# Expert retrieval with dense gate operands and merged token halves in a two-layer decoder trunk

## Chip, cores and metric

One core of a Trainium2 chip. The metric is the device time of one execution of the whole program in microseconds, median of the runs.

## What is computed

Two layers over 256 tokens of width 1024. Each has a mixing sublayer (three head groups, one output projection) and an expert sublayer, each followed by a LayerNorm of the residual. The change concerns the expert sublayer alone:

```python
q = (xc @ wq).reshape(c, PEER_HEADS, 2, half)
sc = jnp.einsum('thid,ikd->thik', q, keys)
top_s, top_i = lax.top_k(sc, PEER_TOPK)
...
gate = jax.nn.softmax(best_s, axis=-1)
ue = u[idx]
ve = v[idx]
act = jax.nn.gelu(jnp.einsum('td,thkd->thk', xc, ue))
return jnp.einsum('thk,thkd->td', (gate * act), ve)
```

There are 128 x 128 experts and 8 x 16 = 128 of them are chosen per token. The kernel does not gather: it multiplies every token with all 16384 expert rows, multiplies the result with a gate that is zero for all but the chosen ones, and multiplies with all value rows.

## The kernel before, in words

**Precision and the weight stream.** All large products are done in three parts of fp32r: the high half of the weights times the high half of the activations, high times low, low times high. Every weight tile of 128 x 1024 comes from HBM (SP's queue, four buffers `raw`), `pump_split` (lines 107 to 122) writes its high half `hi` on ScalarE (L117) and its low half `lo = raw - hi` on VectorE or, for the tiles in `on_pool` (lines 89 to 92), on GpSimd (L118). It runs two tiles ahead of TensorE (`LOOK`); `hi` and `lo` have three buffers each.

**The expert sublayer** (`peer`, lines 821 to 1037). First come the queries and the key scores. Then the *first product*: 128 key blocks j, each one expert tile `("u", l, j)` times the transposed hidden state (`hTh`, `hTl`: 8 chunks of 128 x 256 tokens each), 24 matmuls of 256 columns (`proj_T`, lines 334 to 346). Two blocks share a PSUM bank `acc` of 2 x 256 floats. After each pair `uevac` (line 973) applies the gelu.

Beside the blocks runs background work, written as generators that `bg.step` moves on: `routing` for each half of the tokens (the top-16 searches on VectorE, L846 to L850, then the one-hot work that gives each chosen expert's row and column, `ijT`, and gate, `gT`), and, from about block 55, `wgen` (line 961): 64 gate steps of four tokens, one per block. A step makes one-hot matrices of row and column by comparing with a constant ramp (`gates`, L937, L940, L942, on VectorE), multiplies them on TensorE so that a 128 x 128 gate matrix per token stands in PSUM (`wmm`, two half-float matmuls per token, for the high and the low half of the gate), and multiplies that into `act`, the 128 x 128 x 256 activations (`apply`: L956 on VectorE for the blocks that are already evacuated; L958 on ScalarE writes the bare gate for those to come, and `uevac` then multiplies the gelu into it, L977 and L978).

```python
DVE.tensor_tensor(eq, iota4[:, None, :, :].to_broadcast(sh),
                  ijT[:, :, None, t0:t0 + TG].to_broadcast(sh), op=OP.is_equal)
...
mm(ps[:, i, :], A[:, 0, :, i], eq[:, 1, :, i], True, False)
```

The token is the innermost index of these tiles, so TensorE reads its operands with a step of four half floats.

The *second product* (from line 996) multiplies `act`, split in halves by `gsplit` (L1011 on ScalarE, L1012 on VectorE), with the 128 value tiles in matmuls of 512 columns. The first two pairs of halves live in the buffers of `eq` and `ga`, the others in the space of `hTh` and `hTl`.

**What sets the order.** Each engine executes its instructions in one fixed order, which a scheduler makes when the program is built, from the order in the code and its own idea of when each instruction is ready. So the code does not show where an instruction stands in its engine's queue; the listings in the section on the change do.

Of the kernel before, what the change touches and what calls it, by code (L numbers as in the profile page):

```python
# [46 lines left out]
def trunk(ctx, tc, x, wst, ut, vr, pp_d, rb_d, lnrow, bd_d, keys_d, out):  # L47
# [42 lines left out]
    for l in range(DEPTH):  # L90
        on_pool.update(index["w", l, i] for i in (0, 1, 14, 16, 18, N_IN + N_OUT, N_IN + N_OUT + 1))
        on_pool.update(index["u", l, j] for j in range(4, 110, 3))
# [57 lines left out]
    iota4 = const.tile([128, 128, 4], F16, name="iota4")  # L150
# [19 lines left out]
    def make_consts():  # L170
        POOL.iota(iota4, pattern=[[1, 128], [0, 4]], base=0, channel_multiplier=0, allow_small_or_imprecise_dtypes=True)
# [30 lines left out]
    def layer_norm(h, pool, pre, gb, store, nxt=None, final=False, after=None):  # L202
        """h [128, 2, D] in place, stored to store; returns the transposed split operands."""
# [13 lines left out]
    def layer_norm_(h, pool, pre, g, b, store, nxt, final, after):  # L217
        hT = None
        if not final:
            hTh = hpool.tile([128, KD, SEQ], F32R, name="hTh")  # L220
            hTl = hpool.tile([128, KD, SEQ], F32R, name="hTl")
            hT = (hTh, hTl)
# [84 lines left out]
    # (step, token block, part): r residual and sums, m mean and squares, v variance, n reciprocal root, s centre and  # L307
    # gain, o scale and bias with the transposes, l low halves, p the next weight pieces
# [25 lines left out]
    def proj_T(w, hT, ps, first=False):  # L334
        hi, lo = w
        hTh, hTl = hT
# [22 lines left out]
    def log1p_exp_neg_abs(pool, o, xin, n, tag):  # L359
        """o = max(x, 0) + log1p(exp(-|x|)) on [128, n]"""  # L360
# [32 lines left out]
    def mixer(l, mix, h, hT, pre):  # L393
        hTh, hTl = hT
# [5 lines left out]
        # small per-layer values  # L400
# [31 lines left out]
        # causal depthwise convolution  # L432
# [293 lines left out]
        # projection schedule  # L726
# [60 lines left out]
        # output projection  # L787
# [33 lines left out]
    def peer(l, pool, hT):  # L821
        hTh, hTl = hT
# [29 lines left out]
        def routing(tb):  # L852
# [73 lines left out]
            ACT.activation(gT[:, 1, ts], gr, AF.Copy, scale=LS)  # L926
# [4 lines left out]
        GS, LS = float(2 ** 15), float(2 ** 11)  # L931
# [41 lines left out]
        def uevac(jp_, ps):  # L973
            j = jp_ * 2
            t = state["t"]
            if t > 0:
                ACT.activation(ps[:, :, 0:t], ps[:, :, 0:t], AF.Gelu)  # L977
                DVE.tensor_tensor(act[:, j:j + 2, 0:t], act[:, j:j + 2, 0:t], ps[:, :, 0:t], op=OP.mult)  # L978
            if t < SEQ:
                ACT.activation(act[:, j:j + 2, t:SEQ], ps[:, :, t:SEQ], AF.Gelu)  # L980
# [169 lines left out]
```

## Time and profile before

| | |
|---|---|
| runs | 2100.47, 2103.36, 2103.90 us; median 2103.36 |
| profiled execution, first to last instruction (no other time of it is given) | 2106.6 us |
| busy: TensorE | 2030.2 us |
| busy: VectorE | 1548.2 us |
| busy: ScalarE | 1062.8 us |
| busy: GpSimd | 238.3 us |

How to read it: an engine's busy time is the time in which it executes an instruction; TensorE's matmuls overlap, so its busy time is not a measure of how well it is used. Times in rows are in us from the start of the span, the means of groups in ns. In rows PE is TensorE, PEld its weight loads, DVE VectorE, ACT ScalarE, POOL GpSimd. "[0.21 <-DVE act L956]" behind a row says how long the engine was idle before it and what ended that.

### The profile page before, as it was taken

What the parts mean: (1) busy time and instruction counts of PE and PEld (TensorE: products, weight loads), DVE (VectorE), ACT (ScalarE), POOL (GpSimd) and SP (SyncE); (2) the same over time, 40 slices, a digit from 0 to 9 for tenths busy, and PEclk for the clock granted to TensorE, in tenths of its full rate; (3) what the DMA queues carried; (4) which work ended last, traced back from release to release, by engine and by line L of the source; (5) the groups of instructions that cost most, each with busy time, mean ns of one, the idle gap of its engine ahead of it and who ended that gap; (6) DMA issues with size and microseconds to landing.
All of it is one profiled execution on the core that took longest, in us unless ns stands there. A gap on an engine that the chain in (4) does not pass through costs nothing. (4 is left out here: it accounts for less than half of the span.)

```text
span 2106.6 us, 33808 instructions
## 1 busy us (share of the span) xinstructions
PE 2030.2 (96%) x13212; PEld 1835.5 (87%) x13212; DVE 1548.2 (73%) x2713; ACT 1062.8 (50%) x1523; POOL 238.3 (11%) x120
## 2 busy tenths in 40 slices
PE   7999889999999999999989999899999999999998
PEld 6887889999999888888888769899999998888886
DVE  8786697379999655555687867963999995555555
ACT  5576455454443544444566755554444344444444
POOL 3100122222220000000010001222222200000000
PEclk9999999999999999999999999999999999999999
DMA  6434445544434666666654335455444446666665
GB/s 206 136 110 150 152 152 168 180 141 140 132 130 135 195 194 194 192 194 195 197 180 139 108 133 170 155 173 174 140 132 134 136 151 190 193 196 192 195 195 170
DMA packets 95919, 344.84 MB, mean 164 GB/s; under 512 B 11680, under 2 KB 11952, under 8 KB 95760
## 3 DMA queue, kind: packets, MB, share of 16 engines
q1 hardware_dynamic: 95552, 342.27, 50.3%
q8 instruction: 103, 1.69, 0.3%
q0 software_dynamic: 208, 0.42, 0.1%
q14 instruction: 56, 0.46, 0.1%
HBM read 339.51 MB, written 3.15 MB: 163 GB/s over the span
## 5 line engine op out<-in xcount | busy, mean ns | idle before, releaser
L118 DVE TENSOR_TENSOR lo<-raw,hi 128x1024 fp32r<-128x1024 f32 x544 | 677.5, 1246 | 383.9 <-ACT hi L117 383.5
L117 ACT ACTIVATE hi<-raw 128x1024 fp32r<-128x1024 f32 x630 | 663.8, 1056 | 452.2 <-PE acc L193 342.5
L193 PE MATMUL acc<-hTh,lo 128*128 128x256 f32 x2048 | 581.8, 284 | 20.1 <-DVE lo L118 18.8
L193 PE MATMUL acc<-hTh,hi 128*128 128x256 f32 x2048 | 592.0, 289 | 0.2 <-ACT hi L117 0.2
L193 PE MATMUL acc<-hTl,hi 128*128 128x256 f32 x2048 | 580.1, 283 | 0.0
L193 PEld LDWEIGHTS acc<-hTh,lo 128*128 128x128 f32 x2048 | 392.1, 191 | 24.3 <-DVE lo L118 22.4
L193 PE MATMUL acc<-hi,hTl 128*128 128x512 f32 x1056 | 411.4, 390 | 0.0
L193 PE MATMUL acc<-hi,hTh 128*128 128x512 f32 x1056 | 411.2, 390 | 0.0
L193 PE MATMUL acc<-lo,hTh 128*128 128x512 f32 x1056 | 411.1, 389 | 0.0
L193 PEld LDWEIGHTS acc<-hTh,hi 128*128 128x128 f32 x2048 | 394.3, 193 | 0.7 <-ACT hi L117 0.4
L193 PEld LDWEIGHTS acc<-hTl,hi 128*128 128x128 f32 x2048 | 392.8, 192 | 0.1
L118 POOL TENSOR_TENSOR lo<-raw,hi 128x1024 fp32r<-128x1024 f32 x86 | 223.6, 2602 | 1046.7 <-ACT hi L117 1015.7
L193 PEld LDWEIGHTS acc<-hi,hTh 128*128 128x128 f32 x1056 | 198.3, 188 | 41.6 <-issue 0.7
L193 PEld LDWEIGHTS acc<-hi,hTl 128*128 128x128 f32 x1056 | 198.2, 188 | 41.1
L193 PEld LDWEIGHTS acc<-lo,hTh 128*128 128x128 f32 x1056 | 198.3, 188 | 41.1
L193 PE MATMUL w<-hTh,hi 128*128 128x256 f32 x560 | 161.4, 299 | 7.5 <-DVE y L495 5.7
L1011 ACT ACTIVATE hTh<-act 128x512 fp32r<-128x512 f32 x124 | 77.7, 631 | 166.2 <-PE acc L193 166.2
L1012 DVE TENSOR_TENSOR hTl<-act,hTh 128x512 fp32r<-128x512 f32 x124 | 85.4, 693 | 97.4 <-ACT hTh L1011 97.4
L193 PE MATMUL w<-hTh,lo 128*128 128x256 f32 x560 | 156.9, 289 | 0.0
L193 PE MATMUL w<-hTl,hi 128*128 128x256 f32 x560 | 155.4, 287 | 0.0
L958 ACT ACTIVATE act<-w 128x272 f32<-128x272 f32 (+32 forms) x128 | 61.1, 478 | 146.5 <-DVE act L956 145.8
L193 PE MATMUL w<-eq,ga 128*128 128x128 f16 x512 | 128.0, 294 | 6.9 <-DVE ga L940 6.9
(268 smaller groups left out, 2323.5 us busy)
## 6 DMA issues: line engine op xcount, KB each, us to landing
raw<-in_ut SPq DMA_DIRECT2D x256, 512.0 KB, 3.5
raw<-in_vr SPq DMA_DIRECT2D x256, 512.0 KB, 3.5
raw<-in_wst SPq DMA_DIRECT2D x118, 512.0 KB, 3.5
raw<-in_lnrow SPq DMA_DIRECT2D x8, 512.0 KB, 3.6
hd<-h SPq DMA_DIRECT2D x4, 512.0 KB, 3.9
raw<-hd SPq DMA_DIRECT2D x4, 512.0 KB, 3.5
h<-in_x SPq DMA_DIRECT2D x2, 512.0 KB, 5.7
y<-in_lnrow SPq DMA_DIRECT2D x2, 512.0 KB, 7.0
```

What stands on the lines that cost most here:

```text
L117: ACT.activation(hi, raw, AF.Copy)
L118: (POOL if n in on_pool else DVE).tensor_tensor(lo, raw, hi.bitcast(F32), op=OP.subtract)
L193: PE.matmul(ps, lhsT, rhs, start=start, stop=stop)
L958: ACT.activation(v[:, :, c:128], ps[:, :, c:128], AF.Copy, scale=1.0 / GS)
L1011: ACT.activation(gh, src, AF.Copy)
L1012: DVE.tensor_tensor(gl, src, gh.bitcast(F32), op=OP.subtract)
```

## The change

Five edits in the expert sublayer:

1. The two halves of the hidden state become one tile `hT` with the halves side by side, and a new `proj_U` multiplies the high half of an expert chunk with both in one matmul of 512 columns, and its low half with the high half of the tokens in one of 256. A block now fills a whole PSUM bank: the first 256 columns hold high times high plus low times high, the others high times low.
2. `uevac` therefore copies the second half to SBUF (`us`, ScalarE) and adds the first (VectorE) for each block, and works on the sum in `us`.
3. `gates` makes dense tiles: per token one comparison and two comparisons with product, each a tensor_scalar of 128 half floats with the token's row, column or gate as scalars per partition, from a single ramp `iota1`. 12 instructions on VectorE take the place of 3. The low half of the gate is kept without the factor 2^11, so the third tile that undid it is gone.
4. GpSimd makes the low halves of two expert tiles in three for blocks 2 to 49, where it made those of one in three for blocks 4 to 109 (32 per layer in place of 36).
5. The buffers that the second product borrows first are those of `us` and `ga`, in place of `eq` and `ga`.

```diff
-        on_pool.update(index["u", l, j] for j in range(4, 110, 3))
+        on_pool.update(index["u", l, j] for j in range(2, 50) if j % 3)
...
-            hTh = hpool.tile([128, KD, SEQ], F32R, name="hTh")
-            hTl = hpool.tile([128, KD, SEQ], F32R, name="hTl")
-            hT = (hTh, hTl)
+            hT = hpool.tile([128, KD, 2, SEQ], F32R, name="hT")
+            hTh, hTl = hT[:, :, 0, :], hT[:, :, 1, :]
...
-            eq = pool.tile([128, 2, 128, TG], F16, name="eq", bufs=2)
-            A = pool.tile([128, 3, 128, TG], F16, name="ga", bufs=2)
-            sh = [128, 2, 128, TG]
-            DVE.tensor_tensor(eq, iota4[:, None, :, :].to_broadcast(sh),
-                              ijT[:, :, None, t0:t0 + TG].to_broadcast(sh), op=OP.is_equal)
-            DVE.tensor_tensor(A[:, 0:2], eq[:, 0:1].to_broadcast(sh), gT[:, :, None, t0:t0 + TG].to_broadcast(sh),
-                              op=OP.mult)
-            DVE.tensor_scalar(A[:, 2], eq[:, 1], 1.0 / LS, None, op0=OP.mult)
+            eq = pool.tile([128, TG, 128], F16, name="eq", bufs=2)
+            A = pool.tile([128, TG, 2, 128], F16, name="ga", bufs=2)
+            for i in range(TG):
+                ii, jj = (ijT[:, c, t0 + i:t0 + i + 1] for c in range(2))
+                DVE.tensor_scalar(eq[:, i, :], iota1, jj, None, op0=OP.is_equal)
+                for c in range(2):
+                    DVE.tensor_scalar(A[:, i, c, :], iota1, ii, gT[:, c, t0 + i:t0 + i + 1], op0=OP.is_equal, op1=OP.mult)
...
-                mm(ps[:, i, :], A[:, 0, :, i], eq[:, 1, :, i], True, False)
-                mm(ps[:, i, :], A[:, 1, :, i], A[:, 2, :, i], False, True)
+                for c in range(2):
+                    mm(ps[:, i, :], A[:, i, c, :], eq[:, i, :], c == 0, c == 1)
...
+        def proj_U(w, ps):
+            hi, lo = w
+            for k in range(KD):
+                s = slice(k * 128, (k + 1) * 128)
+                ops = [(ps, hi[:, s], hT[:, k].rearrange("p c t -> p (c t)")), (ps[:, 0:SEQ], lo[:, s], hT[:, k, 0, :])]
+                for i, o in enumerate(ops if k == 0 else ops[::-1]):
+                    mm(*o, k == 0 and i == 0, k == KD - 1 and i == 1)
...
-        def uevac(jp_, ps):
+        def uevac(jp_, pss):
...
+            us = pool.tile([128, 2, SEQ], F32, name="us", bufs=2)
+            for i, ps in enumerate(pss):
+                ACT.activation(us[:, i, :], ps[:, SEQ:2 * SEQ], AF.Copy)
+                DVE.tensor_tensor(us[:, i, :], ps[:, 0:SEQ], us[:, i, :], op=OP.add)
...
-                 for nm, w in (("eq", 512), ("ga", 768))]
+                 for nm, w in (("us", 512), ("ga", 512))]
```

**VectorE, an early gate step of layer 0, before.** L956 is the product of gate and activations, L937, L940 and L942 the gate step, L118 a low half, L978 the product of an evacuated pair.

```order
L956 SCALAR_TENSOR_TENSOR act<-w,act 128x4x60
L937 TENSOR_TENSOR eq<-iota_78,ijT 128x1024 [waits PE_49]
L940 TENSOR_TENSOR ga<-eq,gT 128x1024 [waits DVE_49,PE_49]
L978 TENSOR_TENSOR act<-act,acc 128x2x28 [waits Activation_49]
L942 TENSOR_SCALAR ga<-eq 128x512
L956 SCALAR_TENSOR_TENSOR act<-w,act 128x4x62 [waits Activation_49]
L937 TENSOR_TENSOR eq<-iota_78,ijT 128x1024 [waits PE_49]
L118 TENSOR_TENSOR lo<-raw,hi 128x1024 [waits DMAHW2_49,Activation_49]
```

**The same place in the changed program.** L953 is the product of gate and activations, L986 the addition of the two sums, L937 and L939 the gate step, L989 the product of an evacuated pair.

```order
L953 SCALAR_TENSOR_TENSOR act<-w,act 128x4x60
L986 TENSOR_TENSOR us<-acc,us 128x256
L986 TENSOR_TENSOR us<-acc,us 128x256 [waits Activation_49]
L118 TENSOR_TENSOR lo<-raw,hi 128x1024 [waits DMAHW1_49,Activation_49]
L937 TENSOR_SCALAR eq<-iota_78,ijT 128x128 [waits DVE_49,PE_49]
L989 TENSOR_TENSOR act<-act,us 128x2x28 [waits Activation_49]
L939 TENSOR_SCALAR ga<-iota_78,ijT,gT 128x128 x2
L937 TENSOR_SCALAR eq<-iota_78,ijT 128x128
L939 TENSOR_SCALAR ga<-iota_78,ijT,gT 128x128 x2
```

Two additions have moved in between the gate product and the next low half, and the second of them waits for ScalarE.

**ScalarE at that place, in the changed program.** L985 is the copy of a block's second half, L955 the bare gate for blocks to come, L117 a high half, L988 and L991 the gelu.

```order
L985 ACTIVATE us<-acc 128x256 [waits Activation_49]
L955 ACTIVATE act<-w 128x4x68 [waits DVE_49]
L985 ACTIVATE us<-acc 128x256 [waits PE_49]
L117 ACTIVATE hi<-raw 128x1024 [waits DMAHW3_49]
L988 ACTIVATE us<-us 128x2x28 [waits DVE_49]
L991 ACTIVATE act<-us 128x2x228
```

The copy of a pair's second block stands behind L955, which waits for VectorE; this repeats in every pair of the gate steps.

## Rows read from the trace of the kernel before

**Rows 1.** The page, busy time, share of the span and instructions of each engine.

```profile
PE 2030.2 (96%) x13212; PEld 1835.5 (87%) x13212; DVE 1548.2 (73%) x2713; ACT 1062.8 (50%) x1523; POOL 238.3 (11%) x120
```

**Rows 2.** Table by stretches: length, busy us and instructions per engine, granted clock, DMA.

```profile
core 0: us, PE busy (x) PEld busy (x) DVE busy (x) ACT busy (x) POOL busy (x), PEclk, DMA share, GB/s
254.50:331.30 76.80, 69.39 (x570) 67.69 (x569) 76.73 (x381) 36.93 (x42) 17.91 (x7) 1.00 0.41 138
331.30:431.30 100.00, 97.92 (x829) 97.48 (x827) 45.32 (x61) 50.08 (x61) 27.35 (x11) 0.98 0.56 175
431.30:547.80 116.50, 116.50 (x977) 114.85 (x976) 107.67 (x153) 55.43 (x90) 26.95 (x10) 1.00 0.42 136
547.80:686.30 138.50, 134.76 (x1117) 131.47 (x1116) 134.98 (x178) 57.10 (x107) 21.57 (x8) 1.00 0.41 134
1474.60:1728.70 254.10, 250.96 (x2090) 246.23 (x2089) 241.69 (x330) 112.43 (x196) 49.36 (x18) 1.00 0.41 135
```

**Rows 3.** The same table: first product, second product, and after a long wait.

```profile
350.00:380.00 30.00, 30.00 (x252) 30.00 (x252) 13.09 (x17) 16.32 (x18) 7.28 (x3) 1.00 0.62 190
800.00:850.00 50.00, 50.00 (x223) 41.40 (x222) 29.08 (x29) 24.54 (x28) 0.00 (x0) 1.00 0.61 194
336.70:340.20 3.50, 3.42 (x16) 3.42 (x17) 3.27 (x8) 0.97 (x1) 0.00 (x0) 0.51 0.70 198
```

**Rows 4.** TensorE in order of time: start us, us, instruction, [idle before <-releaser].

```profile
336.78 0.58 PE L193 MATMUL acc<-hTh,lo 128*128 128x256 f32 x1 [2.08 <-DVE lo L118]
...
420.72 1.07 PE L193 MATMUL w<-identb,act 128*128 128x128 bf16 x16
421.60 0.36 PE L193 MATMUL acc<-hTh,hi 128*128 128x256 f32 x1
```

**Rows 5.** VectorE's groups, 431.3 to 686.3 us: busy us, mean ns | idle before.

```profile
L956 DVE SCALAR_TENSOR_TENSOR act<-w,act 128x216 f32<-128x216 f32 (+31 forms) x64 | 61.4, 960 | 2.9 <-ACT act L980 2.8
L940 DVE TENSOR_TENSOR ga<-eq,gT 128x1024 f16<-128x1024 f16 x62 | 61.2, 987 | 0.9
L118 DVE TENSOR_TENSOR lo<-raw,hi 128x1024 fp32r<-128x1024 f32 x47 | 57.5, 1222 | 7.1 <-ACT hi L117 7.1
L937 DVE TENSOR_TENSOR eq<-iota,ijT 128x1024 f16<-128x1024 f16 x62 | 56.8, 916 | 2.7 <-PE w L193 2.6
L942 DVE TENSOR_SCALAR ga<-eq 128x512 f16<-128x512 f16 x62 | 17.8, 287 | 0.0
L978 DVE TENSOR_TENSOR act<-act,acc 128x8 f32<-128x8 f32 (+31 forms) x32 | 13.3, 415 | 0.0
```

**Rows 6.** VectorE in order of time, two places in the mixing sublayer.

```profile
107.76 0.42 DVE L623 TENSOR_SCALAR aa<-rr 128x512 f32<-128x512 f32 x1
108.09 0.42 DVE L621 TENSOR_SCALAR xc<-xc 128x512 f32<-128x512 f32 x1
...
167.35 1.68 DVE L573 TENSOR_SCALAR y<-y,rs_y 128x512 f32<-128x512 f32 x4
```

**Rows 7.** Groups by shape, whole run.

```profile
L287 DVE TENSOR_TENSOR hTl<-w,hTh 128x512 fp32r<-128x512 f32 x16 | 10.4, 682 | 1.0 <-ACT hTh L282 0.8
...
L732 ACT ACTIVATE xp<-w 128x256 f32<-128x256 f32 x24 | 8.6, 366 | 3.7 <-PE w L193 3.7
...
L980 ACT ACTIVATE act<-acc 128x512 f32<-128x512 f32 x54 | 31.4, 582 | 0.1
```

**Rows 8.** VectorE's groups by shape, 64 to 70 us (scalars from `pp`).

```profile
L437 DVE TENSOR_SCALAR xc<-xp,pp 128x256 f32<-128x256 f32 x1 | 0.4, 408 | 0.0
L435 DVE TENSOR_SCALAR xs<-xp,pp 128x256 f32<-128x256 f32 x1 | 0.3, 346 | 0.0
```

**Rows 9.** GpSimd and VectorE in order of time, 517 to 520.7 us.

```profile
517.18 2.94 POOL L118 TENSOR_TENSOR lo<-raw,hi 128x1024 fp32r<-128x1024 f32 x1 [9.96 <-ACT hi L117]
...
518.58 2.10 DVE L940 TENSOR_TENSOR ga<-eq,gT 128x1024 f16<-128x1024 f16 x1
```

**Rows 10.** ScalarE in order of time, the bare gate after VectorE's product.

```profile
524.51 0.54 ACT L958 ACTIVATE act<-w 128x200 f32<-128x200 f32 x1 [0.21 <-DVE act L956]
```

**Rows 11.** ScalarE's groups, 431.3 to 686.3 us.

```profile
L958 ACT ACTIVATE act<-w 128x296 f32<-128x296 f32 (+31 forms) x64 | 30.6, 478 | 74.2 <-DVE act L956 73.8
```

More of the change, by code (lines that the diff above doesn't have):

```diff
@@ L149, in trunk @@
     POOL.tensor_scalar(ident, jp, 0.0, None, op0=OP.is_equal)
-    iota4 = const.tile([128, 128, 4], F16, name="iota4")
+    iota1 = const.tile([128, 128], F16, name="iota1")
     iota16 = const.tile([128, 16, 16], BF16, name="iota16")
@@ L170, in make_consts @@
     def make_consts():
-        POOL.iota(iota4, pattern=[[1, 128], [0, 4]], base=0, channel_multiplier=0, allow_small_or_imprecise_dtypes=True)
+        POOL.iota(iota1, pattern=[[1, 128]], base=0, channel_multiplier=0, allow_small_or_imprecise_dtypes=True)
         POOL.iota(iota16, pattern=[[1, 16], [0, 16]], base=0, channel_multiplier=0, allow_small_or_imprecise_dtypes=True)
@@ L335, in proj_T @@
         hi, lo = w
-        hTh, hTl = hT
+        hTh, hTl = hT[:, :, 0, :], hT[:, :, 1, :]
         if first:
@@ L393, in mixer @@
     def mixer(l, mix, h, hT, pre):
-        hTh, hTl = hT
+        hTh, hTl = hT[:, :, 0, :], hT[:, :, 1, :]
         bg, bg2 = Background(), Background()
@@ L821, in peer @@
     def peer(l, pool, hT):
-        hTh, hTl = hT
         act = pool.tile([128, 128, SEQ], F32, name="act")
@@ L925, in routing @@
             DVE.scalar_tensor_tensor(gr, ps, GS, gT[:, 0, ts], op0=OP.mult, op1=OP.subtract)
-            ACT.activation(gT[:, 1, ts], gr, AF.Copy, scale=LS)
+            ACT.activation(gT[:, 1, ts], gr, AF.Copy)
             yield
@@ L930, in peer @@
         TG = 4
-        GS, LS = float(2 ** 15), float(2 ** 11)
+        GS = float(2 ** 15)
         def gates(t0):
-            eq = pool.tile([128, 2, 128, TG], F16, name="eq", bufs=2)
-            A = pool.tile([128, 3, 128, TG], F16, name="ga", bufs=2)
-            sh = [128, 2, 128, TG]
-            DVE.tensor_tensor(eq, iota4[:, None, :, :].to_broadcast(sh),
-                              ijT[:, :, None, t0:t0 + TG].to_broadcast(sh), op=OP.is_equal)
-            DVE.tensor_tensor(A[:, 0:2], eq[:, 0:1].to_broadcast(sh), gT[:, :, None, t0:t0 + TG].to_broadcast(sh),
-                              op=OP.mult)
-            DVE.tensor_scalar(A[:, 2], eq[:, 1], 1.0 / LS, None, op0=OP.mult)
+            eq = pool.tile([128, TG, 128], F16, name="eq", bufs=2)
[5 more added lines that the diff above has]
+                    DVE.tensor_scalar(A[:, i, c, :], iota1, ii, gT[:, c, t0 + i:t0 + i + 1], op0=OP.is_equal, op1=OP.mult)
             return A, eq
@@ L971, in wgen @@
                 yield
-        def uevac(jp_, ps):
+        def proj_U(w, ps):
[6 more added lines that the diff above has]
+        def uevac(jp_, pss):
             j = jp_ * 2
             t = state["t"]
+            us = pool.tile([128, 2, SEQ], F32, name="us", bufs=2)
+            for i, ps in enumerate(pss):
+                ACT.activation(us[:, i, :], ps[:, SEQ:2 * SEQ], AF.Copy)
+                DVE.tensor_tensor(us[:, i, :], ps[:, 0:SEQ], us[:, i, :], op=OP.add)
             if t > 0:
-                ACT.activation(ps[:, :, 0:t], ps[:, :, 0:t], AF.Gelu)
-                DVE.tensor_tensor(act[:, j:j + 2, 0:t], act[:, j:j + 2, 0:t], ps[:, :, 0:t], op=OP.mult)
+                ACT.activation(us[:, :, 0:t], us[:, :, 0:t], AF.Gelu)
+                DVE.tensor_tensor(act[:, j:j + 2, 0:t], act[:, j:j + 2, 0:t], us[:, :, 0:t], op=OP.mult)
             if t < SEQ:
-                ACT.activation(act[:, j:j + 2, t:SEQ], ps[:, :, t:SEQ], AF.Gelu)
+                ACT.activation(act[:, j:j + 2, t:SEQ], us[:, :, t:SEQ], AF.Gelu)
             state["c"] = j + 2
@@ L987, in peer @@
         for jp_ in range(64):
-            ps = psum.tile([128, 2, SEQ], F32, name="acc", bufs=4)
+            pss = [acc_bank() for _ in range(2)]
             for i in range(2):
-                proj_T(weights(("u", l, jp_ * 2 + i)), hT, ps[:, i, :])
+                proj_U(weights(("u", l, jp_ * 2 + i)), pss[i])
                 bg.step(1 + i if any(g.__name__ == "routing" for g in bg.q) else 1)
-            uevac(jp_, ps)
+            uevac(jp_, pss)
         bg.drain()
@@ L1004, in gslot @@
             if not ring:
-                ring.extend(hpool.tile([128, 4, 2 * SEQ], F32R, name=nm) for nm in ("hTh", "hTl"))
-            return [r[:, jp_ % 4, :] for r in ring]
+                ring.append(hpool.tile([128, 4, 2, 2 * SEQ], F32R, name="hT"))
+            return [ring[0][:, jp_ % 4, i, :] for i in range(2)]
         def gsplit(jp_):
```

## Prediction

> **What bounds the kernel now.** I read the page's busy times first, then a table by stretches, then the groups of VectorE, then single rows. TensorE is busy 96% of the span [rows 1], so one looks for the stretches in which it is not the limit. Both layers have the same stages, so I work on layer 0 and double; the gate stretch of layer 1 took 254.1 us against 255.0 [rows 2].
>
> The stretches that the change touches belong to the first expert product, 128 key blocks ("blocks" below). Read the VectorE column beside the TensorE one [rows 2]. From 254.5 to 331.3 us (the first 20 blocks, top-16 searches beside them) VectorE is busy 76.7 of 76.8 us: it sets the pace. From 331.3 to 431.3 it has half its time free and TensorE paces. From 431.3 to 686.3 (blocks 55 to 120, each with a gate step of four tokens) TensorE is full in the first half, but VectorE has 107.7 and 135.0 of 116.5 and 138.5 us, together 242.7 of 255.0. It is a whisker from being the bound there. That stretch decides this change.
>
> **TensorE's prices.** 252 matmuls of 256 columns in 30 us make 0.119 us each, 223 of 512 columns in 50 us make 0.224 [rows 3]. A block goes from 24 × 0.119 = 2.86 us to 8 × 0.224 + 8 × 0.119 = 2.75. The strided gate matmuls: 977 matmuls in 116.5 us, 32 to a block, make 3.82 us per block [rows 2], so 0.96 for eight. Sixteen dense half-precision ones of the same size go from 420.72 to 421.60 [rows 4], 0.055 each, so eight dense ones should take 0.44. TensorE's need per gate block falls from 3.82 to 3.19 us. Were it the bound, this alone would be worth 41 us a layer.
>
> **VectorE's prices.** Busy times overlap by 0.08 us from one instruction to the next (107.76 + 0.42 against a start at 108.09 [rows 6]), so a term counts its duration less 0.08. An operation of two tensors on 512 floats, one of them in PSUM, takes 0.68 [rows 7], hence 0.60; the 512-float tensor_scalar at twice the rate 0.33 [rows 6]; the difference is half the streaming, so streaming is 0.53 and an instruction starts at 0.07. The half-float tensor_scalar of 512, 0.287 less 0.08 [rows 5], is 0.07 plus a quarter of 0.53: four elements a cycle. For 128 half floats that makes 0.07 + 0.033 = 0.10 us.
>
> Each new gate instruction also takes its scalars per partition from memory. With one such scalar the 512-float form goes from 0.33 to (1.68 − 0.08) / 4 = 0.40 [rows 6]; with a second one the 256-float form goes from 346 to 408 ns [rows 8]. I charge 0.06 per scalar. One comparison (one scalar, 0.16) and two gate products (two scalars, 0.22 each) make 0.60 per token, **2.41 us per gate step**. The old three instructions, without collisions, are 0.60 + 0.60 + 0.21 = 1.41. Bounds for the new step: 12 × 0.10 = 1.2 if scalars were free, 2.8 if two-scalar half-float instructions ran at only twice the rate (0.033 more each). I take 2.41, since both the quadrupled rate and the price of a scalar have rows of their own.
>
> GpSimd's splits: while GpSimd ran 517.18 to 520.12, a gate product that needs 0.68 took 2.10 [rows 9]. Eighteen such splits a layer are gone from this stretch; what they cost VectorE in collisions is already in its old 242.7 us, and the new sum is made without them.
>
> **The gate stretch after.** From the start of block 55 to that of block 121 VectorE, two blocks ahead at its start and none at its end, must do: 64 splits × 1.14 = 73.0 (47 before; GpSimd has none now) [rows 5]; 61 steps × 2.41 = 147.0; 63 gate-to-activation products × (0.96 − 0.08) = 55.4; 32 products of evacuated activations × (0.415 − 0.08) = 10.7 [rows 5]; and the new additions of the two sums, 64 × (0.07 + 0.27) = 21.8. Sum **307.9 us**, 4.8 per block against TensorE's 3.19. VectorE now paces every block, and TensorE's 0.63 us per block is worth nothing.
>
> One wait comes on top. The order rows show it: ScalarE's second copy of a pair stands behind its part of the gate product (L955), which waits for VectorE's part (L953; the old pair shows the same order, 0.21 us idle [rows 10]), and VectorE's second addition, right behind L953 and the first addition, waits for that copy. VectorE's next split and gates stand behind it. So per pair: 0.48 (mean of L958 [rows 11]) + 0.37 (copy of 256 [rows 7]) − 0.41 (first addition beside it) = 0.44, 14 us in 32 pairs. If ScalarE hides it, zero. I take 14. ScalarE itself has room: its 112.5 us here [rows 2] grow by 66 × 0.37 = 24.
>
> Gate stretch: 307.9 + 14 − 255.0 = **+67 us** a layer.
>
> **The other stretches.** Routing: VectorE loses 15 splits (32 of the first 55 go to GpSimd, 17 did) = −17 us, and gains 55 additions × 0.34 = +19. So the first stretch, paced by VectorE, stays; the following 35 blocks, paced by TensorE, gain 0.11 each: −4. Bounds −10 to +15: additions now wait for TensorE in the middle of the searches, and ScalarE's activation waits for them ahead of the next high-half split. The last seven blocks gain 0.8. The second product starts later: its first low half takes the buffer of the last evacuated pair, and so waits for copy 0.37, addition 0.42, activation 0.58 [rows 7], product 0.68 and its own 0.68 [rows 7], less two matmuls of 0.22: +2.3. The second product and the mixer keep their instructions; the halves of the hidden state keep unit stride, nothing changes there.
>
> Per layer 67 − 4 − 0.8 + 2.3 = 64.5; two layers **+129 us**. The profiled execution has a span of 2106.6, so 2236 for its like; the median of the runs stands 3.2 lower, and I say **2232 us**.
>
> **Rivals.** *Scalars cost nothing here* (they are 16-bit and fetched ahead): a step is 1.21, the stretch 307.9 − 73 + 14 = 249, −6 against 255; total 2 × (−6 − 4 + 1.5) = −17, **2086**, and 2058 if the copy's wait is hidden too. Break-even is a step of 1.3 us, 0.109 per instruction; against it stand two independent pairs of rows [rows 6, 8]. The Trainium skill ("VectorE: DVE Perf Modes", the section on the TRN2 errata) speaks for this rival: it gives 58 cycles plus elements over the mode's factor at 0.96 GHz for SBUF to SBUF, 94 ns here, and no charge for a pointer scalar; by it a step would be an estimated 1.13 us, and the kernel some 27 us faster. The trace disagrees: 0.40 us between starts with such a scalar, 0.33 without [rows 6].
>
> *Only twice the rate for half floats with scalars:* 61 × 0.40 = +24 a layer, **2281**.
>
> *ScalarE hides the copy:* −14 a layer, **2204**.
>
> *Routing suffers from the new order,* VectorE waiting for TensorE and TensorE for a late split: +15 instead of −4 a layer, **2270**.
>
> *The clock falls.* After one wait of 2.08 us for a low half [rows 4] the granted clock was 0.51 for the next 3.5 us [rows 3], and TensorE will idle a third of each gate block. At that level 16 matmuls of 256 columns took 3.42 us, 0.21 each [rows 3], so a block would need about 24 × 0.21 + 16 × 0.055 = 5.9 us; if it held through the stretch, 66 × (5.9 − 4.9) = 66 more a layer, **2364**. Against it: the idle time is cut into pieces by the tokens, and a TensorE that is the bound no longer idles. The Trainium skill ("TensorE: Matmul & The Clock Gate", Part 1) calls 1.2 GHz the default, released to 2.4 GHz by activity and taken back by idleness; by it this rival is possible, and the rows agree that one wait brings the level down.
>
> **How the numbers follow.** Forecast 0.60; twice the rate 0.10; copy hidden 0.11; routing worse 0.08; clock 0.04; free scalars 0.07. The range of 2160 to 2290 takes in the first four with the scatter of their terms (a quarter off the price of a scalar is 61 × 20 × 0.015 = 18 us a layer) and leaves out the last two and a little. A difference under 0.2%, 4 us, is about what cannot be told from none; it lies between the free scalars and the rest: 0.02. Faster 0.05, slower 0.93.
>
> **What would show it.** VectorE's busy share near full from about 430 us to the end of the first product; comparisons at some 0.24 us and gate products at 0.30 in the groups; TensorE waiting for the low half and for gate products; block periods near 5 us; VectorE's second addition waiting for the copy; dense gate matmuls near 0.055 us apart. I am wrong if the gate instructions take 0.18 us each, if the gate stretch stays at 255 us or less, or if the time goes elsewhere than into it.

## The result, and the profile after

The changed kernel takes **2245.1 us** (median of 4 runs, 2243.3 to 2248.5) against 2103.6 (4 runs as well): ratio 1.0677, 95% interval 1.0662 to 1.0692. Slower by 141.5 us, where 129 were forecast. The profiled execution has a span of 2242.8 us, 136.2 more than the one before.

Busy times on the page, which answer to [rows 1]:

```profile
PE 2061.0 (92%) x11162; PEld 1650.2 (74%) x11164; DVE 1728.4 (77%) x4129; ACT 1137.6 (51%) x1779; POOL 213.6 (10%) x112
```

TensorE has 2050 matmuls fewer and yet 31 us more busy time, so its busy time does not say what it needs: the same 512-column matmuls have a mean of 429 ns in this kernel's gate stretch and of 405 in that of imm_gates below. VectorE has 180 us more. The table by stretches (columns as in [rows 2]; the first 20 blocks, the next 35, the 66 blocks of the gate steps in layer 0 and in layer 1, and four microseconds in the second product) tells where:

```profile
254.00:319.20 65.20, 59.40 (x322) 49.82 (x321) 65.20 (x324) 37.21 (x54) 31.94 (x12) 0.97 0.45 137
319.20:431.00 111.80, 105.51 (x634) 90.02 (x633) 73.27 (x174) 64.50 (x104) 47.67 (x19) 0.98 0.56 171
431.00:750.00 319.00, 268.29 (x1566) 180.77 (x1562) 312.93 (x969) 132.82 (x261) 0.00 (x0) 1.00 0.36 108
1541.80:1862.30 320.50, 269.23 (x1564) 181.62 (x1561) 312.90 (x969) 132.70 (x261) 0.00 (x0) 0.99 0.36 107
774.90:778.90 4.00, 4.00 (x12) 3.23 (x13) 2.36 (x3) 1.06 (x1) 0.00 (x0) 0.68 0.21 78
```

The gate stretch takes 318.9 us where it took 255.0, and 320.5 where it took 254.1 in layer 1: +64 and +66, nearly the whole loss. VectorE is busy 312.9 us of each. The routing ahead of it kept its time within a microsecond. VectorE's groups in the gate stretch of layer 0 (busy us, mean ns, idle before), against [rows 5]:

```profile
L939 DVE TENSOR_SCALAR ga<-iota,ijT,gT 128x128 f16<-128x128 f16 x496 | 132.6, 307 | 0.0
L118 DVE TENSOR_TENSOR lo<-raw,hi 128x1024 fp32r<-128x1024 f32 x65 | 79.0, 1216 | 0.0
L937 DVE TENSOR_SCALAR eq<-iota,ijT 128x128 f16<-128x128 f16 x248 | 61.4, 247 | 0.7 <-PE w L193 0.7
L953 DVE SCALAR_TENSOR_TENSOR act<-w,act 128x216 f32<-128x216 f32 (+31 forms) x64 | 59.4, 928 | 0.0
L986 DVE TENSOR_TENSOR us<-acc,us 128x256 f32<-128x256 f32 x64 | 23.9, 416 | 0.0
L989 DVE TENSOR_TENSOR act<-act,us 128x8 f32<-128x8 f32 (+31 forms) x32 | 13.6, 425 | 5.8 <-ACT us L988 5.4
```

The gate instructions alone are 194 us busy; before, they were 136, with GpSimd's collisions in it. The last column matters too: no idle time before the additions (L986), 5.8 us before the products of the pairs (L989). In order of time, one step on VectorE:

```profile
599.95 0.55 DVE L939 TENSOR_SCALAR ga<-iota,ijT,gT 128x128 f16<-128x128 f16 x2
600.40 0.27 DVE L937 TENSOR_SCALAR eq<-iota,ijT 128x128 f16<-128x128 f16 x1
600.56 0.55 DVE L939 TENSOR_SCALAR ga<-iota,ijT,gT 128x128 f16<-128x128 f16 x2
601.01 0.97 DVE L953 SCALAR_TENSOR_TENSOR act<-w,act 128x352 f32<-128x352 f32 x1
601.87 0.76 DVE L986 TENSOR_TENSOR us<-acc,us 128x256 f32<-128x256 f32 x2
602.53 1.23 DVE L118 TENSOR_TENSOR lo<-raw,hi 128x1024 fp32r<-128x1024 f32 x1
603.67 0.26 DVE L937 TENSOR_SCALAR eq<-iota,ijT 128x128 f16<-128x128 f16 x1
604.23 0.45 DVE L989 TENSOR_TENSOR act<-act,us 128x280 f32<-128x280 f32 x1 [0.30 <-ACT us L988]
```

From start to start a comparison costs 600.56 − 600.40 = 0.16 us, two gate products 0.45, a token 0.61 and a step of four 2.44. ScalarE at the same place:

```profile
598.83 0.42 ACT L985 ACTIVATE us<-acc 128x256 f32<-128x256 f32 x1
602.01 0.47 ACT L955 ACTIVATE act<-w 128x160 f32<-128x160 f32 x1 [2.76 <-DVE act L953]
602.54 0.39 ACT L985 ACTIVATE us<-acc 128x256 f32<-128x256 f32 x1
602.82 1.05 ACT L117 ACTIVATE hi<-raw 128x1024 fp32r<-128x1024 f32 x1
603.77 0.43 ACT L988 ACTIVATE us<-us 128x280 f32<-128x280 f32 x1
```

The copy behind L955 starts at 602.54, when the second addition is already running. So that addition does not need it: it is the first copy of the *next* pair, and the pair's own second copy was made a step earlier, at 598.83. What VectorE does wait for is the gelu (L988), which stands behind that copy and a high half.

### The profile page after: what moved, and what is told of

Same layout as the page of the kernel before. It is cut to its first block, busy times and chain, and to the rows that moved or that the text cites. A ratio compares the mean times of both kernels' runs of the same rounds, so it can differ in the third digit from the quotient of the medians.

```text
span 2242.8 us, 31342 instructions
## 1 busy us (share of the span) xinstructions
PE 2061.0 (92%) x11162; PEld 1650.2 (74%) x11164; DVE 1728.4 (77%) x4129; ACT 1137.6 (51%) x1779; POOL 213.6 (10%) x112
## 5 line engine op out<-in xcount | busy, mean ns | idle before, releaser
L118 DVE TENSOR_TENSOR lo<-raw,hi 128x1024 fp32r<-128x1024 f32 x552 | 681.1, 1234 | 290.8 <-ACT hi L117 290.2
L117 ACT ACTIVATE hi<-raw 128x1024 fp32r<-128x1024 f32 x630 | 663.7, 1054 | 416.3 <-PE acc L193 316.6
L193 PE MATMUL acc<-hT,hi 128*128 128x512 f32 x2048 | 777.9, 416 | 4.8 <-ACT hi L117 2.6
L193 PE MATMUL acc<-hT,lo 128*128 128x256 f32 x2048 | 590.1, 309 | 117.5 <-DVE lo L118 109.2
L193 PE MATMUL acc<-hi,hT 128*128 128x512 f32 x2112 | 654.0, 390 | 0.0
L193 PEld LDWEIGHTS acc<-hT,lo 128*128 128x128 f32 x2048 | 383.6, 193 | 169.7 <-DVE lo L118 149.1
L193 PEld LDWEIGHTS acc<-hi,hT 128*128 128x128 f32 x2112 | 396.4, 188 | 82.5 <-issue 0.7
L193 PEld LDWEIGHTS acc<-hT,hi 128*128 128x128 f32 x2048 | 385.4, 192 | 67.5 <-ACT act L955 7.7
L193 PE MATMUL acc<-lo,hT 128*128 128x512 f32 x1056 | 411.4, 390 | 0.0
L939 DVE TENSOR_SCALAR ga<-iota,ijT,gT 128x128 f16<-128x128 f16 x1024 | 286.4, 319 | 0.0
L118 POOL TENSOR_TENSOR lo<-raw,hi 128x1024 fp32r<-128x1024 f32 x78 | 199.6, 2565 | 611.4 <-ACT hi L117 603.4
L193 PEld LDWEIGHTS acc<-lo,hT 128*128 128x128 f32 x1056 | 198.4, 188 | 41.0
L193 PE MATMUL w<-hT,hi 128*128 128x256 f32 x1120 | 209.2, 293 | 7.5 <-DVE y L494 5.7
L955 ACT ACTIVATE act<-w 128x272 f32<-128x272 f32 (+32 forms) x128 | 59.8, 467 | 259.1 <-DVE act L953 259.1
L986 DVE TENSOR_TENSOR us<-acc,us 128x256 f32<-128x256 f32 x256 | 99.9, 415 | 47.0 <-ACT us L985 47.0
L937 DVE TENSOR_SCALAR eq<-iota,ijT 128x128 f16<-128x128 f16 x512 | 126.5, 247 | 1.3 <-PE w L193 1.3
```

The source lines that it names most:

```text
L117: ACT.activation(hi, raw, AF.Copy)
L118: (POOL if n in on_pool else DVE).tensor_tensor(lo, raw, hi.bitcast(F32), op=OP.subtract)
L193: PE.matmul(ps, lhsT, rhs, start=start, stop=stop)
L937: DVE.tensor_scalar(eq[:, i, :], iota1, jj, None, op0=OP.is_equal)
L939: DVE.tensor_scalar(A[:, i, c, :], iota1, ii, gT[:, c, t0 + i:t0 + i + 1], op0=OP.is_equal, op1=OP.mult)
L955: ACT.activation(v[:, :, c:128], ps[:, :, c:128], AF.Copy, scale=1.0 / GS)
```

## Experiments

Times are medians; "routing" is layer 0 from block 0 to 55, "gate" from 55 to 121, both by TensorE's first matmul of the block in the profiled execution. Ratios to the kernel before, 95% interval.

| kernel | us | ratio | routing | gate |
|---|---|---|---|---|
| before | 2103.6 | | 176.8 | 255.0 |
| changed | 2245.1 | 1.0662 to 1.0692 | 177.1 | 318.9 |
| imm_gates | 2083.4 | 0.9891 to 0.9924 | 175.8 | 240.4 |
| tt_gates | 2214.3 | 1.0492 to 1.0544 | 176.8 | 301.5 |
| strided_tt | 2097.0 | 0.9961 to 0.9984 | 176.3 | 247.7 |
| old_pool | 2289.6 | 1.0873 to 1.0909 | 168.0 | 350.5 |
| no_pool | 2222.7 | 1.0547 to 1.0595 | 163.8 | 319.1 |
| split_halves_ptr | 2204.8 | 1.0449 to 1.0507 | 190.6 | 290.0 |
| before_pool_routing | 2104.9 | 0.9995 to 1.0026 | 181.2 | 249.7 |
| before_no_pool | 2087.7 | 0.9914 to 0.9948 | 175.7 | 249.7 |
| pairs_split_halves | 2061.8 | 0.9786 to 0.9835 | 181.9 | 228.8 |
| pairs_no_pool | 2043.1 | 0.9691 to 0.9726 | 170.9 | 228.8 |
| pairs_two_instr | 2030.8 | 0.9631 to 0.9670 | 169.7 | 224.7 |
| merge_in_routing | 2019.1 | 0.9577 to 0.9620 | 162.9 | 224.6 |

### What a scalar per partition costs

```diff
-                DVE.tensor_scalar(eq[:, i, :], iota1, jj, None, op0=OP.is_equal)
+                DVE.tensor_scalar(eq[:, i, :], iota1, 3.0, None, op0=OP.is_equal)
...
-                    DVE.tensor_scalar(A[:, i, c, :], iota1, ii, gT[:, c, t0 + i:t0 + i + 1], op0=OP.is_equal, op1=OP.mult)
+                    DVE.tensor_scalar(A[:, i, c, :], iota1, 5.0, 7.0, op0=OP.is_equal, op1=OP.mult)
```

> The changed kernel with constants in place of the scalars per partition in the twelve gate instructions: their number, shapes and places stay, the gates themselves are left out (each compares with and multiplies by the same constants). Theory (VectorE paces the gate stretch, and each scalar that it takes from memory costs 0.06 us): an instruction goes from the 0.16 and 0.225 us between starts in the trace of the changed kernel to about 0.10, a step from 2.44 to 1.2, the stretch from 318.9 to about 242 us, the time to about 2091 us. Rival A (the price is that of an instruction, whatever its scalars): 2245. Rival B (TensorE, the copies or the additions set the block, the gates run beside them): 2235 to 2245.

2083.4 us, 8 below the theory's number and 162 below the changed kernel. VectorE in order of time:

```profile
562.06 0.30 DVE L939 TENSOR_SCALAR ga<-iota 128x128 f16<-128x128 f16 x2
562.26 0.20 DVE L937 TENSOR_SCALAR eq<-iota 128x128 f16<-128x128 f16 x1
562.37 0.30 DVE L939 TENSOR_SCALAR ga<-iota 128x128 f16<-128x128 f16 x2
562.57 0.19 DVE L937 TENSOR_SCALAR eq<-iota 128x128 f16<-128x128 f16 x1
```

Without a scalar from memory 0.10 to 0.11 us an instruction (562.26 to 562.37, and 0.20 for two products); with one 0.16, with two 0.225: **0.06 us a scalar**, twenty a step. The number of instructions is the same, so rival A falls; the merge is the same, so rival B falls.

### The same tiles in two instructions

```diff
-            eq = pool.tile([128, TG, 128], F16, name="eq", bufs=2)
-            A = pool.tile([128, TG, 2, 128], F16, name="ga", bufs=2)
...
+            eq = pool.tile([128, 2, TG, 128], F16, name="eq", bufs=2)
+            A = pool.tile([128, 2, TG, 128], F16, name="ga", bufs=2)
+            sh = [128, 2, TG, 128]
+            DVE.tensor_tensor(eq, iota1[:, None, None, :].to_broadcast(sh),
+                              ijT[:, :, t0:t0 + TG, None].to_broadcast(sh), op=OP.is_equal)
+            DVE.tensor_tensor(A, eq[:, 0:1].to_broadcast(sh), gT[:, :, t0:t0 + TG, None].to_broadcast(sh), op=OP.mult)
...
+                    mm(ps[:, i, :], A[:, c, i, :], eq[:, 1, i, :], c == 0, c == 1)
```

> The changed kernel with the same dense gate tiles made by two tensor_tensor of 1024 half floats, the token's row, column and gate repeated along the innermost axis as second tensor. Theory: only VectorE's price of the step counts. If such an operand goes at two elements a cycle, as the token-interleaved one did, a step is 1.2 us and the kernel 2091; if a repeated innermost element takes it to one a cycle, a step is 2 x 1.13 = 2.27 and the kernel about 2224. Rival A (number of instructions): 2 for 12, 2091 or below. Rival B (the merge sets the block): 2235 to 2245. TensorE's gate matmuls stay at 0.055 in each.

2214.3 us: the theory's slower branch, 10 below its 2224. VectorE's groups in its gate stretch, and below them those of the next kernel, whose tiles have four tokens innermost:

```profile
L935 DVE TENSOR_TENSOR eq<-iota,ijT 128x1024 f16<-128x1024 f16 x62 | 75.7, 1221 | 0.7 <-PE w L193 0.7
L937 DVE TENSOR_TENSOR ga<-eq,gT 128x1024 f16<-128x1024 f16 x62 | 75.7, 1220 | 0.0
```

```profile
L935 DVE TENSOR_TENSOR eq<-iota,ijT 128x1024 f16<-128x1024 f16 x62 | 43.3, 698 | 6.5 <-PE w L193 5.8
L937 DVE TENSOR_TENSOR ga<-eq,gT 128x1024 f16<-128x1024 f16 x62 | 43.1, 696 | 0.4
```

The repeated innermost element halves the rate. The Trainium skill ("Advanced Engine Details and Errata", VectorE Performance Modes) names unit stride as a condition of the doubled rate for 16-bit data; these rows agree, 1221 ns with a repeated innermost element and 698 without. Two instructions for twelve gained 31 us only, so the count is not what costs; imm_gates, which keeps the count, says the same.

### Token-interleaved tiles under the merged product

```diff
+            eq = pool.tile([128, 2, 128, TG], F16, name="eq", bufs=2)
+            A = pool.tile([128, 2, 128, TG], F16, name="ga", bufs=2)
...
+                    mm(ps[:, i, :], A[:, c, :, i], eq[:, 1, :, i], c == 0, c == 1)
```

> The changed kernel with token-interleaved gate tiles again, made by the two tensor_tensor of before (the third instruction, which undid a factor, is not needed). Theory: a step is 1.2 us, VectorE's stretch 242, but TensorE is back at 0.118 for each strided gate matmul, 8 x 0.224 + 8 x 0.119 + 0.96 = 3.71 a block or 245 us for 66: both near the bound, 245 to 252 a layer, 2097 to 2112 us. Rival A: below that by nothing, the same number. Rival B (the merged product with its copies and additions is what costs): over 2200.

2097.0, at the lower edge of the theory's range and 148 us below the change: with the old tiles (and without the third of the old gate instructions) the same merge, copies and additions lose nothing. Now TensorE sets the stretch:

```profile
426.90:674.60 247.70, 247.26 (x1563) 213.78 (x1561) 239.45 (x349) 130.43 (x261) 0.00 (x0) 1.00 0.46 138
```

### Where GpSimd splits

```diff
-        on_pool.update(index["u", l, j] for j in range(2, 50) if j % 3)
+        on_pool.update(index["u", l, j] for j in range(4, 110, 3))
```

> The changed kernel with GpSimd's splits where they were before (18 a layer in the gate stretch, 17 in the routing). Theory: each split saves VectorE 1.14 us in the gate stretch and costs it some 1.5 to 1.9 in collisions (the gate products beside GpSimd in the routing of the changed kernel take 0.70 in place of 0.31 us): +6 to +14 a layer, 2257 to 2273 us. Rival (the splits that GpSimd gave up are what VectorE lacks): 18 x 1.14 = 20 a layer less, 2204.

2289.6: the sign was right, the size was not. The kernel loses 44 us where 12 to 28 were expected; the gate stretch grew by 31.6 (350.5), while the routing shrank by 9.1 (168.0), which nobody expected. Its three stretches, one collision, and GpSimd's instruction at that time:

```profile
249.40:309.40 60.00, 57.26 (x323) 48.63 (x322) 60.00 (x287) 38.21 (x55) 14.80 (x6) 1.00 0.49 150
309.40:417.40 108.00, 105.38 (x636) 89.96 (x634) 79.26 (x229) 64.04 (x102) 31.18 (x12) 0.98 0.56 175
417.40:767.90 350.50, 289.11 (x1565) 201.88 (x1562) 328.83 (x951) 132.49 (x261) 45.38 (x18) 0.90 0.33 98
```

```profile
574.79 2.36 POOL L118 TENSOR_TENSOR lo<-raw,hi 128x1024 fp32r<-128x1024 f32 x1 [16.21 <-ACT hi L117]
...
575.03 2.38 DVE L989 TENSOR_TENSOR act<-act,us 128x232 f32<-128x232 f32 x1 [0.19 <-ACT us L988]
```

```profile
L989 DVE TENSOR_TENSOR act<-act,us 128x8 f32<-128x8 f32 (+31 forms) x32 | 28.0, 876 | 21.4 <-ACT us L988 21.4
```

VectorE's 0.4 us product lasts as long as GpSimd's split. Eighteen splits fewer are 18 × 1.14 = 20.5 us less, yet VectorE's sum rises by 15.9: 2.0 us lost for each. With 15.6 us more of waits for the gelu (21.4 against 5.8), which the expectation did not count, that is the whole 31.6. The granted clock fell as well, to 0.90 over the stretch, where the changed kernel has 1.00; since VectorE is busy or waits for the gelu throughout, what that cost can only lie inside those waits. The Trainium skill says in the section named above ("Advanced Engine Details and Errata", VectorE Performance Modes) that VectorE's second port into SBUF is shared with GpSimd, and that GpSimd's instructions and VectorE's two-port ones block each other. The row shows such a block, though of a tensor_tensor, for which that section's table has no two-port mode; the tensor_scalar rows of the kernel without the merge, below, are of a kind that has one.

```diff
-        on_pool.update(index["u", l, j] for j in range(2, 50) if j % 3)
```

> The changed kernel with no low half of the first product on GpSimd; the gate stretch keeps its code, the 32 splits of the routing come back to VectorE. Theory (a split on GpSimd costs the routing more than it saves, 0.6 us each by the 9.1 us that 15 of them made): routing 158 to 168 in place of 177 us, 2207 to 2227. Rival (VectorE lacks the time in the searches; 13 of the splits lie there): +15 us a layer, 2275.

2222.7, within the theory's range. 0, 17 and 32 splits on GpSimd in the routing make it 163.8, 168.0 and 177.1 us. VectorE had the time, and TensorE then runs almost without a gap:

```profile
256.00:314.10 58.10, 56.84 (x323) 48.74 (x321) 58.07 (x238) 37.99 (x55) 0.00 (x0) 1.00 0.52 154
314.10:419.80 105.70, 104.35 (x636) 88.60 (x634) 94.42 (x294) 64.21 (x104) 0.00 (x0) 1.00 0.61 180
```

More splits on GpSimd did not mean a shorter first stretch: the changed kernel does 324 instructions of VectorE in its first 20 blocks, this one 238, so the searches were only done earlier. How much of the 13 us is collisions and how much this other order stays open, as no run changes one without the other. The same in the kernel before, first the change's own line:

```diff
-        on_pool.update(index["u", l, j] for j in range(4, 110, 3))
+        on_pool.update(index["u", l, j] for j in range(2, 50) if j % 3)
```

> The kernel before with GpSimd's splits where the change puts them, and nothing else of it. Theory (GpSimd's splits beside VectorE cost it more than they save, in the routing too: with 17 in place of 32 there the changed kernel's routing took 168.0 in place of 177.1 us): gate stretch VectorE 65 x 1.14 + 62 x 1.41 + 56 + 11 = 229 us without collisions, so TensorE sets it, 66 x 3.83 = 253, -2 a layer; routing +5 to +9 a layer; together 2109 to 2117. Rival (as forecast: the routing gains or keeps its time): 2095 to 2100.

2104.9, between the two: the gate stretch gained 5.3 (249.7; most blocks take the theory's 3.83 us, but three of the 66 have no gate step and take 2.9), the routing lost 4.4. Edit 4 alone is worth nothing that can be told from none (0.9995 to 1.0026). Then without any such line:

```diff
-        on_pool.update(index["u", l, j] for j in range(4, 110, 3))
```

> The kernel before with no low half of the first product on GpSimd, and nothing else of the change. Theory (each of those splits costs more than it saves, in both stretches): gate stretch 249.7 us as with GpSimd in the routing only, routing from 181 to between 158 (55 blocks x 2.88, TensorE alone) and 172: 2059 to 2087. Rival (VectorE lacks the time in the searches of the first 20 blocks): +7 a layer for the 6 splits there, 2110 or more.

2087.7: the gate stretch as expected, 249.7, but the routing at 175.7, worse than 158 to 172. So here the 17 splits of the routing cost 1 us only, against 4 in the changed kernel. Between blocks 20 and 55 the longest wait of TensorE was 2.3 us, for a low half, and the granted clock was 0.97 over these 114 us. The time is a microsecond above the range; one line removed makes the kernel before 0.7% faster.

### The merged product alone

The diff is that of `proj_U` and `uevac`, reversed:

```diff
-            pss = [acc_bank() for _ in range(2)]
+            ps = psum.tile([128, 2, SEQ], F32, name="acc", bufs=4)
...
-                proj_U(weights(("u", l, jp_ * 2 + i)), pss[i])
+                proj_T(weights(("u", l, jp_ * 2 + i)), hT, ps[:, i, :])
```

> The changed kernel without the merged product: the 24 matmuls of 256 columns of before, no copies, no additions, the gelu straight from PSUM; dense gates and GpSimd's places as in the change. Theory (VectorE's sum sets the gate stretch): 64 additions x 0.34 = 22 us and up to 6 us of waits for the gelu less a layer, the routing within 4 us; TensorE's 24 x 0.119 + 0.44 = 3.30 a block stays below VectorE's 4.4. 2245 - 2 x (22 to 28) = 2189 to 2201. Rival (the merge saves TensorE time that counts, 0.11 us in each of 128 blocks): 2245 + 28 = 2273 at most, 2240 to 2273.

2204.8, some 4 above the theory's range. The gate stretch gained 28.9 us, about what the additions (22) and the wait for the gelu (6) are worth. The routing lost 13.5, which nobody expected. Both kernels have the gate instructions of the first steps in the middle of the routing, beside GpSimd; what differs is where VectorE's next low half stands. In this kernel it stands behind the collisions, and TensorE waits for it:

```profile
360.89 4.69 POOL L118 TENSOR_TENSOR lo<-raw,hi 128x1024 fp32r<-128x1024 f32 x2 [3.19 <-ACT hi L117]
...
360.97 2.37 DVE L941 TENSOR_SCALAR ga<-iota,ijT,gT 128x128 f16<-128x128 f16 x1
363.26 2.38 DVE L939 TENSOR_SCALAR eq<-iota,ijT 128x128 f16<-128x128 f16 x1
...
366.61 1.21 DVE L118 TENSOR_TENSOR lo<-raw,hi 128x1024 fp32r<-128x1024 f32 x1
...
367.88 0.58 PE L193 MATMUL acc<-hTh,lo 128*128 128x256 f32 x1 [5.76 <-DVE lo L118]
```

In the changed kernel it stands ahead of them:

```profile
356.92 1.22 DVE L118 TENSOR_TENSOR lo<-raw,hi 128x1024 fp32r<-128x1024 f32 x1
358.05 4.83 DVE L939 TENSOR_SCALAR ga<-iota,ijT,gT 128x128 f16<-128x128 f16 x2
...
358.19 0.51 PE L193 MATMUL acc<-hT,lo 128*128 128x256 f32 x2 [0.98 <-DVE lo L118]
```

Instructions that cost 0.225 and 0.16 us elsewhere take 2.3 to 2.4 in both. The kernel without the merge has a second such wait, of 5.39 us, at 332 us, behind two collisions of the routing's own instructions; the longest wait in the changed kernel's routing is 2.54. So these waits come from the order of VectorE's queue, which changes with every edit here, and not from the missing merge as such.

These kernels split the change's 141.5 us in one order of steps: edit 4 alone +1.3 (2103.6 to 2104.9), then the dense gates +99.9 (to 2204.8), then merge, copies, additions and the other buffers +40.3. In another order the parts have other sizes: with GpSimd's old places (old_pool) the changed kernel would have lost 44 us more, so there edit 4 is worth 44.

### Dense enough for both engines

Two tokens innermost: VectorE's second operand then repeats over pairs, and TensorE reads with a step of two half floats.

```diff
+            eq = pool.tile([128, 2, TG // 2, 128, 2], F16, name="eq", bufs=2)
+            A = pool.tile([128, 2, TG // 2, 128, 2], F16, name="ga", bufs=2)
+            sh = [128, TG // 2, 128, 2]
...
+            for c in range(2):
+                DVE.tensor_tensor(eq[:, c], iota2[:, None, :, :].to_broadcast(sh), per_token(ijT, c), op=OP.is_equal)
+            for c in range(2):
+                DVE.tensor_tensor(A[:, c], eq[:, 0], per_token(gT, c), op=OP.mult)
...
+                    mm(ps[:, i, :], A[:, c, i // 2, :, i % 2], eq[:, 1, i // 2, :, i % 2], c == 0, c == 1)
```

> Neither kernel's gates: tiles with two tokens innermost in place of four or one, made by four tensor_tensor of 512 half floats; product and evacuation as before the change, GpSimd's places as in the change. Theory: an operand repeated over pairs still goes at two elements a cycle (repeated over single elements it went at one: 1.14 us between starts for 1024), a step is 4 x 0.34 = 1.36, VectorE 74 + 84 + 56 + 11 = 225 a gate stretch; a TensorE operand with a step of two lies between 0.055 and 0.118, 2.86 + 0.44 to 0.96 a block, 218 to 252. So 225 to 252 a stretch in place of 255, with the routing 0 to 9 longer: 2043 to 2115, and below 2075 if the step of two goes at full pace. Rival (pairs fall to one element a cycle): a step of 2.4, VectorE 290, 2170 to 2190.

2061.8 us, faster than the kernel before by 41. VectorE kept the doubled rate (418 ns for 512 half floats, 0.34 us between starts), and TensorE the pace of dense operands: its eight gate matmuls take 0.44 us from the first to what follows them, as in this row of pairs_two_instr, which reads the same tiles with the same step:

```profile
539.41 0.63 PE L192 MATMUL w<-eq,ga 128*128 128x128 f16 x8
539.85 0.36 PE L192 MATMUL acc<-hTh,hi 128*128 128x256 f32 x1
```

That is 0.055 each, as the dense ones in [rows 4]. Then GpSimd's splits out, by the edit of no_pool:

> The two-token gate tiles with the old product, and no split of the first product on GpSimd. Theory: gate stretch 229 us as it was with these tiles, routing from 181.5 to between 158 and 172: 2062 - 2 x (10 to 23) = 2016 to 2042. Rival (the searches lack VectorE): 2062 or more.

2043.1, a microsecond above the theory's range; the routing (170.9) gained 11, near the lower of the bounds of 10 and 23. Then four instructions made two: row, column and gate of four tokens lie together in `ijT` and `gT`, and one tensor_tensor of 1024 does each kind.

```diff
-        ijT = pool.tile([128, 2, SEQ], F16, name="ijT")
+        ijT = pool.tile([128, SEQ // 4, 2, 4], F16, name="ijT")
...
+                v = t[:, t0 // TG].rearrange("p c (g s) -> p (c g) s", s=2)
+                return v[:, :, None, :].to_broadcast([128, TG, 128, 2])
+            DVE.tensor_tensor(eq.rearrange("p c g j s -> p (c g) j s"),
+                              iota2[:, None, :, :].to_broadcast([128, TG, 128, 2]), per_token(ijT), op=OP.is_equal)
```

> The same with two tensor_tensor of 1024 half floats in place of four of 512 (row, column and gate of four tokens lie together, operands of four dimensions). Theory: two starts of 0.07 less a step, VectorE 226 - 62 x 0.14 = 217 a gate stretch, TensorE 66 x 3.31 = 218.5: both at 218 to 224, 10 to 20 us below the kernel with four. Rival (operands of four dimensions go at one element a cycle or start late): 2.3 a step, +55 a layer.

2030.8: 12 below, within the expected 10 to 20. Its gate stretch:

```profile
424.30:648.90 224.60, 223.40 (x2091) 220.09 (x2089) 219.03 (x288) 115.83 (x197) 0.00 (x0) 1.00 0.44 153
```

TensorE is full again and most blocks take 3.40 us, 0.52 more than the 2.88 without gates, where four tokens innermost add 0.95 (3.83). Last, the merge where TensorE sets the pace and VectorE has time:

```diff
+            if jp_ < MERGED:
+                pss = [acc_bank() for _ in range(2)]
+            else:
+                pss = psum.tile([128, 2, SEQ], F32, name="acc", bufs=4)
...
+                if jp_ < MERGED:
+                    proj_U(w, pss[i])
+                else:
+                    proj_T(w, hT, pss[:, i, :])
```

> The fastest kernel so far (two-token gate tiles in two instructions, no split of the first product on GpSimd, 2030.75 us) with the merged product, its copies and additions for the first 52 blocks alone, where VectorE has time to spare. Theory (the merge pays where TensorE sets the pace and VectorE has room for the additions): the routing as in the changed kernel without GpSimd's splits, 163.8 in place of 169.7 us, the gate stretch at 224.7 as before, the second product without a longer start, since its first buffers are not those of the sums: 2031 - 2 x 6 = 2019, between 2014 and 2024. Rival (the additions and copies cost the routing what the merge saves): 2028 to 2040.

**2019.1 us**, 4.0% below the kernel before (0.9577 to 0.9620). Its routing and gate stretch:

```profile
249.30:307.40 58.10, 56.80 (x322) 48.74 (x321) 58.07 (x238) 37.98 (x55) 0.00 (x0) 1.00 0.45 155
307.40:412.20 104.80, 104.37 (x659) 89.78 (x658) 91.39 (x272) 63.58 (x102) 0.00 (x0) 1.00 0.52 181
412.20:636.80 224.60, 223.44 (x2092) 220.17 (x2090) 218.99 (x288) 115.95 (x197) 0.00 (x0) 1.00 0.44 153
```

TensorE is busy over 97% of all three. So the merge is worth 12 us here (2030.8 to 2019.1, intervals of the ratios apart): the idea was sound; its place was not.

## Why the prediction was right

**The bound.** The forecast rested on VectorE being a whisker from the bound in the gate stretch and becoming it. It did, and the stretch came out at +64 and +66 us where +67 stood.

**The gate step.** 2.41 us was forecast from rows of another sublayer [rows 6, 8]; measured: 2.44. The rival of free scalars needed 0.10 per instruction; imm_gates shows those 0.10 when the scalars are gone, and 162 us less.

**VectorE's sum.** 307.9 forecast, 312.9 measured: 62 steps of 2.44 in place of 61 of 2.41 (+4.3) and one split more (+1.1).

**The wait of the second addition: wrong.** 14 us a layer were charged to the copy behind L955. The rows above show no idle time at the additions, because the copy that is behind the L955 in question belongs to the next pair, and the pair's own second copy, a step earlier, has long been made. The section on the change reads it the same wrong way. The order rows were read without asking which tile each copy writes. VectorE waits 5.8 us elsewhere, for the gelu. Sum and wait together were 321.9 against 318.9, so two errors of opposite sign cancelled to 3 us.

**Routing: the step that failed.** −4 was forecast and about 0 came. The first 20 blocks stayed, as forecast (65.5 us before, 65.2 after; the prediction's stretch to 331.3 us is longer than it says, as block 20 starts at 320.0 and block 23 at 331.3). The −4 of the following 35 did not come: 111.8 us after 111.3. TensorE's waits for low halves there, from 320.0 to 431.3 us before and from 319.2 to 431.0 after:

```profile
L193 PE MATMUL acc<-hTh,lo 128*128 128x256 f32 x281 | 80.6, 287 | 3.3 <-DVE lo L118 3.3
...
L193 PE MATMUL acc<-hT,lo 128*128 128x256 f32 x280 | 73.8, 284 | 6.2 <-DVE lo L118 4.6 <-POOL lo L118 1.5
```

They account for 2.9 of the 4 us. The sum credited each split handed to GpSimd in full, "VectorE loses 15 splits = −17 us", and counted no wait for it; in the changed kernel the routing took 177.1 us with 32 splits there, 168.0 with 17 and 163.8 with none. That the bounds of −10 to +15 held is no merit of the step.

**The second product's start.** +2.3 forecast. TensorE waited 3.19 us for the low half in the borrowed buffer, and then came what the forecast named only as a rival for the gate stretch:

```profile
771.31 0.39 PE L193 MATMUL acc<-lo,us 128*128 128x512 f32 x1
774.89 1.42 PE L193 MATMUL acc<-hi,us 128*128 128x512 f32 x5 [3.19 <-DVE us L1023]
```

In the four microseconds that followed, the granted clock was 0.68 and 12 matmuls were done, which at 0.224 each take 2.7: 1.3 more, 4.5 in all.

**The clock rival** did not come in the gate stretch of the changed kernel (1.00 and 0.99), but it did in old_pool's (0.90), where most blocks with a split on GpSimd take 7 to 10 us and TensorE waits longer in one piece than in the changed kernel (up to 2.3 us against 1.6).

**The 13 us between 2232 and 2245.** Per layer the gate stretch came out 2 below the forecast, the routing 4, the last blocks 0.5 and the rest 1 above: 7 in both layers. The other 5 to 6 are in how the profiled executions stand to their medians: the one before lay 3.2 above, the one after 2.3 below.

**Smaller slips.** The break-even step of 1.3 us holds for the gate stretch alone; with the other terms it is 1.35. The rival of twice the rate charges all twelve instructions, though its bound speaks of the eight with two scalars.

## What to carry to other kernels

Cost an added VectorE instruction by start, streaming and its scalars from memory, not by its size: here 0.07, 0.03 and 0.06 each (the first two as the prediction works them out; their sum, 0.10, was measured), so that half of a gate step was the price of its scalars. Before handing work to GpSimd to relieve VectorE, ask what VectorE runs beside it: here a split in the gate stretch cost VectorE 2.0 us and saved it 1.14, and in all three kernels in which their number was varied fewer splits on GpSimd made the routing shorter. When an operand's layout sets two engines against each other, look for the step that both take at full rate, as the pair of half floats did, and put a saving of one engine only into the stretch in which that engine is the bound.

## What was not expected of the hardware

- A scalar per partition costs VectorE 0.06 us even at 16 bits: 0.10, 0.16 and 0.225 us for 128 half floats with none, one and two.
- Eight half-float matmuls of 128 columns add 0.52 us to a block when their operands are read with a step of two elements, which is the pace of dense ones, and 0.95 with a step of four.
- One VectorE instruction of 128 half floats lasted 2.38 us beside a GpSimd split, although it needs 0.16; it ended with the split (365.64 against 365.58 us).
- Whether the scalars' price is a read of its own or a slower start was not tried; the runs show only that it is per scalar.
